# SSD decay exponents and skip term as TensorE products, and four steps stored or moved anew, in a one-core hybrid streaming step

## The chip, the cores and the metric

One core of one Trainium2 chip runs the whole program. The metric is the device time of one execution in microseconds. The kernel before took 1944.94 us (the median of three runs, from 1942.18 to 1947.05).

## The reference, cut to what matters

One layer for 1024 prompt rows and 8 streams of 16 new rows each (nine blocks of 128 rows). Three token mixers read the same projection `u @ w_in`: stick-breaking attention ("sb", 4 heads), forgetting attention ("fox", 4 heads) and a state-space mixer (SSD, 8 heads in 2 groups). Their outputs are put side by side and go through `w_out`; a cross-attention and a SwiGLU FFN follow. The change touches the SSD, the forget-gate sums of the sample rows, and the seam between mixers and `w_out`:

```python
seg = a_cum[:, :, :, None, :] - a_cum[:, :, None, :, :]
decay = jnp.exp(jnp.where(causal[None, None, :, :, None], seg, -jnp.inf))
scores = jnp.einsum('bcthn,bcshn->bctsh', C, B) * decay
y_diag = jnp.einsum('bctsh,bcshp->bcthp', scores, x)
...
y = (y + p['d_skip'].astype(jnp.float32)[:, None] * xs).reshape(b, n, SSD_INNER).astype(u.dtype)
...
fcum = jnp.cumsum(jnp.concatenate([past['fox_logf'].astype(jnp.float32), logf], axis=1), axis=1)
s = s + (jnp.transpose(fq, (0, 2, 1))[..., :, None] - jnp.transpose(fk, (0, 2, 1))[..., None, :])
...
out = jnp.einsum('bne,ed->bnd', mix, p['w_out'])
```

## The kernel before, in words

All is fp32. A large product runs as three TensorE products on a high and a low part of each operand (`mm3`, lines L314, L315, L316); TensorE transposes by a product with the identity. Each engine (PE, DVE, ACT, POOL) works its instructions strictly in the order in which a scheduler put them before the run, from the order and priorities of the code; SP issues every DMA, in one order too, and an issue that waits holds up those behind it. On-chip tiles come from pools with few slots: `ring` has three slots each for tags `wh` and `wl` (two for `wr`), `psd`, `pss`, `pst` are PSUM banks (2, 2, 3), `sgp` has four slots, `actp` six large ones. A tile whose pool is full waits until the last reader of the slot's former owner is done.

The stages in order: memory projection, norm and first projections (to about 120 us of the profile); the attention pipeline, in which the units of the sb heads and then the fox heads run, each pair of streams of the sample rows as one decode unit between them; beside the pipeline, step by step at a set rate, the generator `fill` gives PE other work: first the remaining projections (`fill_s`), and from about 545 us on the SSD (`ssd_gen`). `heads_out` starts with `w_out` beside the last steps, `finish_rows` adds the SSD's part, and cross-attention and FFN follow from 880 us to the end.

The places that the change touches:

- **Sample gate sums**, `fox_sums` in `fill_s`. Running sums of 32 rows (stream, head) over 1024 past and 16 new places are made by scans on DVE (L687), written to DRAM as `fs_sc` with 16 copies of each row (`fssc<-xc`), and read back by each fox decode unit as a bias. A last small product with `hsel` (L696) needs a DVE result (`so`, L692). Then `z_proj` and others follow (L314 to L316 with 264 columns).
- **SSD chunk.** Nine chunks, the sample chunk 8 first, then 0 to 7, each in four parts. `load(i)`: x, B, C of the chunk from `xbc_sc` (L998), the running sums of the gate, 8 heads of 128 values, broadcast to 128 partitions from `ac_sc` (L1000, `act<-acsc`, 512 KB written), and z (L1002). `prepare`: transposes (L1015, L1019), then products with per-head columns on POOL (`heads_tt`, L991), the skip term `xD` with `hb` among them. `weights`: B·C per group on PE (L1030), times the causal mask on DVE (L1032); the difference of running sums, clamped at zero, per head on ACT (L1038, 3 heads) or DVE (L1040, 5 heads); the exponential on ACT (L1043); times the masked B·C on DVE (L1046). `states`: the state's part of y and the new state (L1055, L1061; in chunk 8 per stream, L1092 to L1108, from two loads `act<-state_ssm` of 1024 KB that are issued there). Its last line adds xD on POOL. `outputs`: the products with x (L1118), the sum (L1120), times z on POOL, the norm (L1125). `write`, one chunk late: four transposes (L1130) and two stores to `mix_sc` (L1134).
- **Fox decode.** K of two streams comes in halves through `wr`, is transposed (L856) and copied by ACT (L857) into `kf`, tags `wh` and `wl` of the ring; V comes in halves as `vr` straight into the same two tags (L905), read by 64 small products (L896: 32 for each unit, beside 4 with the new rows).
- **The seam.** `load_rows` brings the heads' rows from `mix_sc` (L1311) when the last of them are stored (L596 stores one head's part); `add_rows` walks the nine blocks with four k each, `act<-mixsc` (L1320) brings the SSD's part.

Of the kernel before, what the change touches and what calls it, by code (L numbers as in the profile page):

```python
# [8 lines left out]
F32 = mybir.dt.float32  # L9
# [8 lines left out]
P = 128  # L18
# [22 lines left out]
NACT = 3  # L41
FSC, CBE = "D", "DD"
# [20 lines left out]
def tile_hybrid_step(ctx: ExitStack, tc: tile.TileContext, a: dict):  # L63
# [177 lines left out]
    fs_sc = dram([32, DEC_S, PAST + DEC_S], F32, "fssc")  # L241
    ac_sc = dram([72, P], F32, "acsc")
# [403 lines left out]
    def fox_sums():  # L646
# [164 lines left out]
    def decode_units(m):  # L811
# [15 lines left out]
        def rows(p):  # L827
# [47 lines left out]
            SP.dma_start(out=fkb[:, :PAST], in_=fs_sc[8 * p:8 * p + 8, :, :PAST].rearrange("i t k -> (i t) k"))  # L875
# [51 lines left out]

    def ssd_gen():
# [8 lines left out]
        avx = sc[:, 1944:2456]  # L937
        ndsk = hb[:, 20:28]
# [37 lines left out]
        at = sg2_t()  # L976
        DVE.tensor_copy(at[:72, :P], ps[:72, :P])
        SP.dma_start(out=ac_sc, in_=at[:72, :P])
# [16 lines left out]

        def load(i):
# [3 lines left out]
            SP.dma_start(out=A[:, 1024:2048],  # L1000
                         in_=ac_sc[8 * i:8 * i + 8, :].rearrange("h t -> (h t)").unsqueeze(0).to_broadcast([P, 1024]))
# [8 lines left out]
        def prepare(i, A, B):  # L1010
# [12 lines left out]
            heads_tt(xD, xn, ndsk)  # L1023

        def weights(i, A, B):
            xT, br, zt, Bn, cb, xn, xd, xe, xD = views(A, B)

            ps = pd()
            for g in range(2):
                PE.matmul(ps[:, g * P:(g + 1) * P], xT[:, 4 + g, :], xT[:, 6 + g, :], start=True, stop=True)  # L1030
            msk = triu if i < 8 else btri
            DVE.tensor_tensor(out=cb.rearrange("p (g t) -> p g t", g=2), in0=ps[:, :256].rearrange("p (g t) -> p g t", g=2),  # L1032
                              in1=msk.unsqueeze(1).to_broadcast([P, 2, P]), op=ALU.mult)

            for h in range(8):
                e, a_s = br[:, h * P:(h + 1) * P], acum[:, 8 * i + h:8 * i + h + 1]
                if h < NACT:
                    ACT.activation(e, e, AF.Relu, bias=a_s, scale=-1.0)  # L1038
                else:
                    DVE.tensor_scalar(e, e, a_s, 0.0, ALU.subtract, ALU.min)  # L1040
            for h0, h1, sgn in ((0, NACT, -1.0), (NACT, 8, 1.0)):
                if h1 > h0:
                    ACT.activation(br[:, h0 * P:h1 * P], br[:, h0 * P:h1 * P], AF.Exp, scale=sgn)  # L1043
            for g in range(2):
                b3 = br[:, g * 512:(g + 1) * 512].rearrange("p (h t) -> p h t", h=4)
                (DVE if CBE[g] == "D" else POOL).tensor_tensor(out=b3, in0=b3, in1=cb[:, g * P:(g + 1) * P].unsqueeze(1).to_broadcast([P, 4, P]),  # L1046
                                  op=ALU.mult)

        def states(i, A, B, t1):
# [14 lines left out]
            else:  # L1064
                hs_, cps = [], []
                for g in range(2):
                    t = act_t(F32)
                    hst = t[:, :2048].rearrange("p (u n) -> p u n", n=P)
                    SP.dma_start(out=hst, in_=a["state_ssm"][0, 4 * g:4 * g + 4].rearrange("b h p n -> (b h p) n")
                                 .rearrange("(u p) n -> p u n", p=P))  # L1070
# [41 lines left out]
            pool_tt(t1, t1, xD, ALU.add)  # L1112

        def outputs(i, A, B, t1):
            xT, br, zt, Bn, cb, xn, xd, xe, xD = views(A, B)
            ps = pd()
            for h in range(8):
                PE.matmul(ps[:, h * 64:(h + 1) * 64], br[:, h * P:(h + 1) * P], xd[:, h * 64:(h + 1) * 64],  # L1118
                          start=True, stop=True)
# [19 lines left out]
        B = act_t(F32)  # L1139
        prepare(order[0], A, B)  # L1140
# [3 lines left out]
        for n, i in enumerate(order):  # L1144
# [20 lines left out]
            last = (i, t1)  # L1165
            if n < 8:
# [4 lines left out]
        write(*last)  # L1171
# [750 lines left out]
```

## Time and profile before

| quantity | value |
|---|---|
| three runs | 1942.18, 1944.94, 1947.05 us |
| the profiled execution, its own time | 1950.47 us |
| its span in the profile | 1948.8 us |
| its mean granted TensorE clock | 0.979 |
| DMA moved in 560 to 760 us | 51.94 MB |
| DMA `act<-acsc` | 9 of 512 KB each |
| DMA `fssc<-xc` | 1 of 2080 KB |

The profile's page gives busy time by engine and, in 40 slices, how busy each is and which TensorE clock was granted. The table of windows does the same for any stretch of time. The waits of PE name, for each line, what ended the idle time ahead of it. The groups by line and form give count, busy time and mean of one, and the idle time before them by what ended it. The chain that ended last follows the run back from its end; a piece of it is the time in which nothing else could have been late. PE overlaps neighbouring instructions, so what a product costs is the distance between the starts of two, not its duration; an fp32 product that isn't one of the three rounded parts leaves two records.

### The profile page before, as it was taken

The numbers are of one execution on the slowest core, as the hardware profiler recorded it, in microseconds if no ns is written. First come the engines' busy times: TensorE is split into PE (matmuls) and PEld (weight loads), VectorE is DVE, ScalarE is ACT, GpSimd is POOL, SyncE is SP. The second block draws the span as 40 slices with busy tenths as digits, with TensorE's granted clock in tenths as the row PEclk, the third lists the DMA queues.
The fourth block names the chain that finished last, engine by engine and source line by source line (L and its number), as shares of the span: only waits on it lengthen the run. The fifth ranks groups of instructions, "written<-read, shape, count | busy, mean of one in ns | idle before, by whom it ended". The sixth has DMA issues, their size and how long they took to land.

```text
span 1948.8 us, 32126 instructions
## 1 busy us (share of the span) xinstructions
PE 1848.2 (95%) x12128; PEld 1647.8 (85%) x12128; DVE 898.4 (46%) x1802; ACT 818.2 (42%) x1702; POOL 629.8 (32%) x918
## 2 busy tenths in 40 slices
PE   7989997999888888999999999999999999999997
PEld 5889776898876665889998888999999999888886
DVE  3421324466645883254444377433333333445554
ACT  6431543445656772143333165333332333344443
POOL 6632405263424552321101212644444443000000
PEclk9999997999999898999999999999999999999999
DMA  9355756445487789234559123332223323556572
GB/s 340 130 168 153 218 122 155 132 137 166 137 241 239 240 273 331 87 115 141 166 165 367 64 96 99 98 74 68 69 68 95 75 68 87 193 189 232 180 243 88
DMA packets 325754, 307.52 MB, mean 158 GB/s; under 512 B 88540, under 2 KB 288324, under 8 KB 325600
## 3 DMA queue, kind: packets, MB, share of 16 engines
q1 hardware_dynamic: 325600, 305.48, 51.2%
q8 instruction: 95, 1.56, 0.3%
q14 instruction: 59, 0.48, 0.1%
HBM read 229.31 MB, written 76.11 MB: 157 GB/s over the span
## 4 chain that ended last, share of the span: by engine, by line
PE 78%; DMA 6%; DVE 4%; POOL 2%; ACT 2%; issue 1%; SPq 0%; DVEq 0%; POOLq 0%; ACTq 0%
PE psd L1789 11%; PE psd L314 10%; PE psd L315 10%; PE psd L316 10%; PE pst L1789 8%; PE pss L1789 4%; PE pss L314 2%; PE pss L315 2%; PE pss L316 2%; PE pso L1789 2%; PE pst L314 2%; PE pst L315 2%; PE pst L316 2%; PE pso L580 1%; PE pst L856 1%
## 5 line engine op out<-in xcount | busy, mean ns | idle before, releaser
L132 POOL TENSOR_TENSOR wl<-wr,wh 128x256 fp32r<-128x256 f32 (+1 forms) x180 | 139.4, 808 | 241.1 <-ACT wh L289 185.0
L314 PE MATMUL psd<-act,wh 128*128 128x384 f32 x576 | 197.7, 344 | 5.3 <-DVE sg L441 2.6
L315 PE MATMUL psd<-act,wh 128*128 128x384 f32 x576 | 196.7, 341 | 0.0
L316 PE MATMUL psd<-act,wl 128*128 128x384 f32 x576 | 196.4, 341 | 0.1
L1789 PE MATMUL pst<-bT,tr 128*128 128x256 f32 (+1 forms) x1068 | 155.0, 293 | 0.0
L316 PE MATMUL psd<-wh,act 128*128 128x512 f32 (+3 forms) x464 | 152.5, 330 | 0.0
L314 PE MATMUL psd<-wh,act 128*128 128x512 f32 (+3 forms) x446 | 146.8, 333 | 4.3 <-ACT wh L289 1.9
L315 PE MATMUL psd<-wl,act 128*128 128x512 f32 (+3 forms) x446 | 146.6, 329 | 0.0
L1789 PEld LDWEIGHTS pst<-bT,tr 128*128 128x128 f32 x1068 | 144.9, 188 | 0.1
L1789 PE MATMUL psd<-bT,tr 128*128 128x320 f32 (+1 forms) x912 | 133.2, 295 | 0.8 <-DVE tr L1636 0.5
L251 POOL TENSOR_SCALAR sm<-sm 128x1 f32<-128x1 f32 (+2 forms) x30 | 11.0, 368 | 378.3 <-ACT y L1884 291.5
L1789 PEld LDWEIGHTS psd<-bT,tr 128*128 128x128 f32 x912 | 124.7, 188 | 1.8 <-DVE tr L1636 0.7
L314 PEld LDWEIGHTS psd<-act,wh 128*128 128x128 f32 x576 | 108.7, 189 | 9.4 <-DVE sg L441 3.0
L132 POOL TENSOR_TENSOR tr<-u,tr 128x256 fp32r<-128x256 f32 x110 | 82.6, 780 | 101.1 <-ACT tr L1632 83.3
L132 POOL TENSOR_TENSOR ws<-ws 128x256 f32<-128x256 f32 (+2 forms) x100 | 73.0, 759 | 116.3 <-DVE ws L507 86.6
L316 PEld LDWEIGHTS psd<-act,wl 128*128 128x128 f32 x576 | 108.5, 188 | 2.0 <-issue 1.3
L315 PEld LDWEIGHTS psd<-act,wh 128*128 128x128 f32 x576 | 108.8, 189 | 0.9 <-issue 0.6
L1764 DVE TENSOR_TENSOR tr<-tr,pst 128x256 f32<-128x256 f32 (+1 forms) x86 | 38.6, 449 | 139.4 <-ACT tr L1761 106.1
L314 PEld LDWEIGHTS psd<-wh,act 128*128 128x128 f32 x446 | 85.6, 192 | 14.2 <-ACT wh L289 2.1
L132 POOL TENSOR_TENSOR tr<-raw,tr 128x256 fp32r<-128x256 f32 x94 | 69.4, 768 | 84.6 <-ACT tr L1632 76.4
L316 PEld LDWEIGHTS psd<-wh,act 128*128 128x128 f32 x464 | 89.0, 192 | 8.7 <-issue 1.3
L289 ACT CAST wh<-wr 128x1024 fp32r<-128x1024 f32 (+2 forms) x45 | 47.1, 1051 | 111.3 <-PE psd L316 48.1
(590 smaller groups left out, 4617.4 us busy)
## 6 DMA issues: line engine op xcount, KB each, us to landing
u<-w_down SPq DMA_DIRECT2D x40, 512.0 KB
raw<-w_down SPq DMA_DIRECT2D x26, 512.0 KB
st<-qksc SPq DMA_DIRECT2D x48, 256.0 KB
wr<-w_in SPq DMA_DIRECT2D x22, 512.0 KB
tr<-hidsc SPq DMA_DIRECT2D x57, 192.0 KB
hidsc<-tr SPq DMA_DIRECT2D x34, 288.0 KB
qksc<-sg SPq DMA_DIRECT2D x48, 192.0 KB
wr<-cache_sb_k SPq DMA_DIRECT2D x16, 512.0 KB
```

The source lines that it names most:

```text
L132: POOL.tensor_tensor(out=out[:, a0:a1], in0=in0[:, a0:a1], in1=in1[:, a0:a1], op=op)
L251: POOL.tensor_scalar(v, ss, inv, EPS, ALU.mult, ALU.add)
L289: ACT.copy(hi[:, :n], raw[:, :n])
L314: PE.matmul(out, ah, bh, start=start, stop=False)
L315: PE.matmul(out, ah, bl, start=False, stop=False)
L316: PE.matmul(out, al, bh, start=False, stop=stop)
L580: return PE.matmul(po[r:r + 64, q_], vt[:, 2 * (k0 + i) + j, :], pfs[i][:, sl], start=start and k0 == 0 and (j == 0 or qp > 0), stop=k0 + ...
L856: PE.transpose(tp[:, k * P:(k + 1) * P], rv[:, k, nb * P:(nb + 1) * P], ident)
L1764: DVE.tensor_tensor(out=at(out, g), in0=at(x, g), in1=ps[g][:, :GW[g]], op=op)
L1789: PE.matmul(dst[g][:, :GW[g]], x[:, ka], y[:, k, :], start=start and k == 0 and m == 0, stop=stop and k == 3 and m == 2, skip_group_check= ...
```

## The change

- `fox_sums` writes two copies of each row instead of 16 (260 KB for 2080 KB) and the decode units read them with a broadcast; after the scan and the stores it hands PE four steps of `z_proj(0)` before its last product.
- SSD decay. The negated running sums are split in a high and a low part and stored to `ac_sc`. Per chunk three small loads bring them to `mv` (10 rows of 1024) and `kv` (10 rows of 256), beside rows of ones and indicators loaded once from the new `ind_sc`. Per group of four heads PE makes the exponent in a `pst` bank: one product puts the mask there (512 columns), one of depth 10 adds the differences (512 columns). ACT takes the exponential straight from PSUM, DVE multiplies with B·C, which stays in its `psd` bank (`cp`). L1032, L1038, L1040 and the broadcast load go. `mv` takes two of the three `wh` slots of the ring for the length of the SSD, `kv` and the sample mask one of the three `wl` slots.
- Skip term. POOL builds diag(d_skip) once (4 operations); per chunk four fp32 products of 128 x 128 put the skip term into the bank of y, and the eight products with x add to it. 18 operations of L991 and 18 additions on POOL go.
- The states of the 8 streams come in eight loads of 256 KB right behind the loads of the first chunk instead of two of 1024 KB in `states`.
- The last chunk's `write` is put off until 12 more steps of `heads_out` have been given out; `add_rows` runs the first two k of a block three blocks ahead of its last two, in banks of `psd` and `pss` in turn.

```diff
-        SP.dma_start(out=fs_sc, in_=sr.unsqueeze(1).to_broadcast([32, DEC_S, PAST + DEC_S]))
+        SP.dma_start(out=fs_sc, in_=sr.unsqueeze(1).to_broadcast([32, 2, PAST + DEC_S]))
         for p in range(4):
             SP.dma_start(out=fqs[:, p:p + 1], in_=fs_sc[8 * p:8 * p + 8, 0, PAST:PAST + DEC_S])
+        yield
+        for _ in range(NZ):
+            yield next(z)
...
+        mv = [ring.tile([P, 1056], F32R, tag="wh", name="wh")[0:10, :1024] for _ in range(2)]
+        cr = ring.tile([P, 1056], F32R, tag="wl", name="wl")
+        kv = [cr[0:10, 256 * x:256 * x + 256] for x in range(2)]
+        mask8 = cr[:, 512:640]
...
-            SP.dma_start(out=A[:, 1024:2048],
-                         in_=ac_sc[8 * i:8 * i + 8, :].rearrange("h t -> (h t)").unsqueeze(0).to_broadcast([P, 1024]))
+            SP.dma_start(out=f32(mv_[0:2]), in_=f32(ac_sc[:, 8 * i:8 * i + 8, :].rearrange("x h t -> x (h t)")))
+            for x in range(2):
+                SP.dma_start(out=f32(kv_[2 + 4 * x:6 + 4 * x]).rearrange("h (g t) -> h g t", g=2),
+                             in_=f32(ac_sc[x, 8 * i:8 * i + 8, :]).rearrange("(g h) t -> h g t", h=4))
...
-            heads_tt(xD, xn, ndsk)
...
-                if h < NACT:
-                    ACT.activation(e, e, AF.Relu, bias=a_s, scale=-1.0)
+                if i < 8:
+                    PE.matmul(p3, mask_fx, identr.unsqueeze(1).to_broadcast([P, 4, P]), start=True, stop=False)
                 else:
-                    DVE.tensor_scalar(e, e, a_s, 0.0, ALU.subtract, ALU.min)
...
+                PE.matmul(ps, sums[i][1][:, g * P:(g + 1) * P], sums[i][0][:, sl], start=False, stop=True)
...
+                ACT.activation(br[:, sl], pss_[g], AF.Exp)
...
-            pool_tt(t1, t1, xD, ALU.add)
...
+            for j in range(4):
+                PE.matmul(ps[:, j * P:(j + 1) * P], xT[:, j, :], skip[:, j * P:(j + 1) * P], start=j == 0, stop=False,
+                          skip_group_check=True)
...
+        st8 = [act_t(F32) for _ in range(2)]
+        for b in range(8):
+            SP.dma_start(out=st8[b // 4][:, 512 * (b % 4):512 * (b % 4 + 1)].rearrange("p (u n) -> p u n", n=P),
+                         in_=a["state_ssm"][0, b].rearrange("h p n -> (h p) n").rearrange("(u p) n -> p u n", p=P))
...
+            if n == 8:
+                final.append(lambda: write(i, t1))
...
-        write(*last)
-        yield
...
+        zs = [z_proj(i) for i in range(2)]
+        yield from fox_sums(zs[0])
...
+            for blk in range(NBLK + ahead):
+                if blk < NBLK:
+                    half(blk, 0)
+                    yield
+                if blk >= ahead:
+                    half(blk - ahead, 2)
+                    yield
...
+    for _ in range(12):
+        next(ho, None)
+    final[0]()
```

The order of instructions on PE behind the small product of `fox_sums` (L685 before), in the kernel before. L547, L548 and L550 are scores of an sb head; L696 is the last small product, L756 belongs to the padding that follows:

```order
L685 MATMUL psd<-fold,so 32x16
L547 MATMUL pss<-st 128x128
L548 MATMUL pss<-st 128x128
L550 MATMUL pss<-mask_sb,identr 128x128
L547 MATMUL pss<-st 128x256
L548 MATMUL pss<-st 128x256
L550 MATMUL pss<-mask_sb,identr 128x128
L547 MATMUL pss<-st 128x384
L548 MATMUL pss<-st 128x384
L550 MATMUL pss<-mask_sb,identr 128x128
L696 MATMUL psd<-so,hsel 128x128
```

The same place on PE in the changed kernel, tiles numbered; `wh_3090` and `wl_3091` are the first weight unit of `z_proj(0)`, `wh_3101` and `wl_3102` the second:

```order
L314 MATMUL psd_3109<-wh_3090,act_350 128x264
L547 MATMUL pss_3351<-st_3141,st_3140 128x128
L548 MATMUL pss_3351<-st_3142,st_3140 128x128
L550 MATMUL pss_3351<-mask_sb_123,identr_119 128x128
L315 MATMUL psd_3109<-wl_3091,act_350 128x264
L316 MATMUL psd_3109<-wh_3090,act_351 128x264
L314 MATMUL psd_3109<-wh_3101,act_350 128x264
L547 MATMUL pss_3366<-st_3141,st_3140 128x256
L548 MATMUL pss_3366<-st_3142,st_3140 128x256
L550 MATMUL pss_3366<-mask_sb_123,identr_119 128x128
L314 MATMUL psd_3169<-wh_3090,act_350 128x264
```

Between the 32 x 16 product and the first that reads `wl_3102`, 26 products of `z_proj` now stand among the head's scores; before, all of them stood behind L696.

The second fox decode unit of those that run beside the SSD, on PE in the kernel before (L896 reads the V halves, L1030, L1055, L1061 are the SSD's):

```order
L1030 MATMUL psd<-act 128x128 x2
L1055 MATMUL psd<-act 128x256 x2
L896 MATMUL pso<-pt,act 32x128 x4
L896 MATMUL pso<-vr,act 32x128 x32
L1061 MATMUL psd<-act 128x256 x2
```

The same unit on PE in the changed kernel (L902 is the line that was L896; L1154 are the skip products, L1157 those with x, L1169 the transposes of `write`, L1071 the B·C products):

```order
L902 MATMUL pso<-pt,act 32x128 x4
L902 MATMUL pso<-vr,act 32x128 x17
L1154 MATMUL psd<-act 128x128 x4
L1157 MATMUL psd<-act 128x64 x8
L1169 MATMUL psd<-ident,sg 128x128 x4
L902 MATMUL pso<-vr,act 32x128 x15
L1071 MATMUL psd<-act 128x128 x2
```

The 32 products of one piece have become 17 and 15 with work of the SSD between them; three of the four fox decode units are split so.

More of the change, by code (lines that the diff above doesn't have):

```diff
@@ L975, in ssd_gen @@
         PE.transpose(ps[:72, :P], acum, ident)
-        at = sg2_t()
-        DVE.tensor_copy(at[:72, :P], ps[:72, :P])
-        SP.dma_start(out=ac_sc, in_=at[:72, :P])
+        t = sg2_t(F32R)
+        an = [t[0:72, P * x:P * x + P] for x in range(2)]
+        ACT.activation(an[0], ps[:72, :P], AF.Copy, scale=-1.0)
+        DVE.scalar_tensor_tensor(an[1], ps[:72, :P], -1.0, f32(an[0]), ALU.mult, ALU.subtract)
+        for x in range(2):
+            SP.dma_start(out=f32(ac_sc[x]), in_=f32(an[x]))
+        DVE.tensor_scalar(mask8, btri, -1.0, -NEG, ALU.add, ALU.mult)
+        for j in range(4):
+            POOL.tensor_tensor(out=skip[:, j * P:(j + 1) * P].rearrange("p (h d) -> p h d", d=64),
+                               in0=ident.rearrange("p (h d) -> p h d", d=64),
+                               in1=ndsk[:, 2 * j:2 * j + 2].unsqueeze(2).to_broadcast([P, 2, 64]), op=ALU.mult)
         POOL.memset(hT, 0.0)
@@ L994, in heads_tt @@
                                    op=ALU.mult)
+        sums, loads = {}, [0]
         def load(i):
@@ L1035, in weights @@
-            for h in range(8):
-                e, a_s = br[:, h * P:(h + 1) * P], acum[:, 8 * i + h:8 * i + h + 1]
-                if h < NACT:
-                    ACT.activation(e, e, AF.Relu, bias=a_s, scale=-1.0)
-                else:
[L1040 to L1043, printed above, removed]
+                PE.matmul(cp[:, g * P:(g + 1) * P], xT[:, 4 + g, :], xT[:, 6 + g, :], start=True, stop=True)
@@ L1065, in states @@
                 hs_, cps = [], []
-                for g in range(2):
-                    t = act_t(F32)
+                for g, t in enumerate(st8):
                     hst = t[:, :2048].rearrange("p (u n) -> p u n", n=P)
-                    SP.dma_start(out=hst, in_=a["state_ssm"][0, 4 * g:4 * g + 4].rearrange("b h p n -> (b h p) n")
-                                 .rearrange("(u p) n -> p u n", p=P))
                     cp = t[:, 2048:3072]
@@ L1252, in tile_hybrid_step, with add_rows @@
             acc -= 1.0
-    def add_rows(w, k0, rows, h):
+    def add_rows(w, k0, rows, h, ahead=0):
         for j in range(2):
@@ L1328, in heads_out @@
         more_h(NBLK)
-        yield from add_rows(a["w_out"][0], 0, lambda k, b: [t[:, b * P:(b + 1) * P] for t in rows[k]], h)
+        yield from add_rows(a["w_out"][0], 0, lambda k, b: [t[:, b * P:(b + 1) * P] for t in rows[k]], h, 3)
     ho = heads_out()
     weave(fill, ho, WV, "ho")
+    for _ in range(12):
+        next(ho, None)
+    final[0]()
     ch = [chunk_t() for _ in range(NCH)]
```

67 lines of the change are left out of this document (43 added, 24 removed).

## The prediction

> **What bounds the kernel now.** I read the page first: who is busy, and what the chain that ended last is made of.
>
> ```profile
> span 1948.8 us, 32126 instructions
> PE 1848.2 (95%) x12128; PEld 1647.8 (85%) x12128; DVE 898.4 (46%) x1802; ACT 818.2 (42%) x1702; POOL 629.8 (32%) x918
> PE 78%; DMA 6%; DVE 4%; POOL 2%; ACT 2%; issue 1%; SPq 0%; DVEq 0%; POOLq 0%; ACTq 0%
> ```
>
> TensorE is busy 95% of the span and holds 78% of the chain; no other engine comes near it. So work that is added to PE costs its full price except where PE stands still or is slowed, and work that is taken from DVE, ACT, POOL or DMA gains only where PE waits for it. Hence the windows next: where does PE stand still?
>
> ```profile
> core 0: us, PE busy (x) PEld busy (x) DVE busy (x) ACT busy (x) POOL busy (x), PEclk, DMA share, GB/s
> 312.00:320.00 8.00, 7.87 (x44) 7.75 (x43) 2.68 (x6) 1.76 (x5) 5.78 (x12) 0.57 0.98 199
> 566.00:576.00 10.00, 4.90 (x25) 4.60 (x25) 3.77 (x12) 4.12 (x10) 4.31 (x6) 0.66 0.95 281
> 616.00:618.00 2.00, 2.00 (x11) 2.00 (x11) 1.08 (x6) 0.61 (x2) 1.68 (x7) 0.50 1.10 303
> 580.00:747.00 167.00, 147.73 (x1200) 111.36 (x1198) 120.47 (x338) 116.12 (x255) 87.16 (x138) 0.95 0.82 257
> 747.00:764.00 17.00, 9.38 (x30) 6.76 (x30) 3.89 (x10) 2.33 (x6) 5.76 (x10) 0.70 0.99 323
> 1180.00:1949.00 769.00, 755.52 (x4797) 704.31 (x4796) 340.01 (x585) 282.61 (x556) 228.71 (x312) 0.99 0.41 121
> ```
>
> The long last stage (FFN) has PE busy throughout at full clock, and the change leaves it alone. The chunks of the SSD, 580 to 747 us, are different: PE is busy 147.73 of 167 us, so 19.3 us idle, and at a granted clock of 0.95, which is another 7.4 us (5% of 147.73) lost to a slow clock. These 26.7 us are all that this stretch can give. Around it lie three short holes (from 304, at 566, at 747 us), each followed by a stretch at a low clock. Whom PE waits for there, the waits say:
>
> ```profile
> PE psd L696 <- DVE so L692: 6.4, 1, 6.4
> PE pst L1092 <- DMA act<-state_ssm: 4.8, 1, 4.8
> PE psd L1130 <- DVE sg L1125: 4.2, 1, 4.2
> PE pst L856 <- DMA wr<-cache_fox_k: 3.8, 2, 2.8
> PE pso L896 <- DMA vr<-cache_sb_v: 3.6, 2, 1.9
> PE psd L1015 <- DMA act<-xbcsc: 3.0, 3, 1.7
> PE psd L1055 <- DVE act L1032: 2.9, 3, 1.7
> PE psd L314 <- DMA ws<-mixsc: 2.7, 1, 2.7
> PE pss L547 <- ACT xc L686: 1.3, 1, 1.3
> ```
>
> Each of the four moves aims at one of these rows: the sums at L696, the states at L1092, the last write at L1130 and `ws`; the SSD's new exponent does away with L1032.
>
> **The gate sums.** PE stood 6.4 us before L696 and 1.3 us before L547. What follows it ran on a half clock:
>
> ```profile
> 313.49 0.42 PE L315 MATMUL psd<-wl,act 128*128 128x264 f32 x1
> 313.71 0.42 PE L316 MATMUL psd<-wh,act 128*128 128x264 f32 x1
> ```
>
> One 264-column product then starts each 0.22 us. The order puts 26 of them ahead of the second weight unit's low part, 26 x 0.22 = 5.7 us of work out of the slow stretch into the hole. They cannot close it: the second unit's low half is made on POOL behind operations that wait for the same DVE scans, so PE stands still again until about where it did. From nothing (the products find no operands in time) to all of hole and slow clock (6.4 + 1.3 + 7.87 x 0.43 = 11.1), I take 5, somewhat less than the 5.7. The smaller store, 260 KB for 2080 KB, shortens a DMA that no row here waits for: nothing; the cover is the time until the first fox decode unit, and if that were gone it could gain, not lose.
>
> **The states.** Hole 4.8 us, slow clock after it 4.90 x 0.34 = 1.7: 6.5 at most. The wait goes, but what is late next stands in the same queue:
>
> ```profile
> 561.79 9.88 DMA act<-state_ssm
> 219.10 7.97 DMA vr<-cache_sb_v
> 743.13 7.95 DMA mixsc<-sg
> 751.13 7.09 DMA ws<-mixsc
> ```
>
> A load takes 7 to 10 us when the engines are full (DMA share 0.95 in the window of 566). The 2 MB now go ahead on SP of the indicator store, its four loads, the store of the split sums and the small loads, and the first exponent product waits for that whole chain. I take a gain of 1, between a loss of 2 and 6.5.
>
> **The seam.** The last head's store and its load back take 7.95 + 7.09 = 15 us in the chain, whatever PE does. In that time the changed order has 15 products of `w_out` before the first that reads that head, where 9 stood, and the four skip products of the last chunk: 6 x 0.23 + 4 x 0.23 (both prices below) = 2.3 us of cover gained; the bounds are nothing and the whole hole with its clock (4.2 + 2.7 + 9.38 x 0.30 = 9.7). The deferred write is hidden behind some hundred products of `w_out`.
>
> **The SSD on PE.** Per chunk two mask and two exponent products of 512 columns, and four fp32 products of 128 x 128. Prices, from neighbours of the same shape:
>
> ```profile
> 748.02 0.39 PE L315 MATMUL psd<-wl,ws 128*128 128x512 f32 x1
> 748.25 0.39 PE L316 MATMUL psd<-wh,ws 128*128 128x512 f32 x1
> 663.77 0.46 PE psd L1030 x4
> ```
>
> One starts 0.23 us after the other; and four records of L1030, which are two products, hold the chain for 0.46, so 0.23 each. 36 x 0.23 + 36 x 0.23 = 16.6 us added to PE. What lies beside idle time: PE's pieces in the chain between 580 and 747 us come to about 67 of 167 us, 40% (my sum over its pieces; five of them are quoted in this part and the ring's). By that share 6.6 us land on the path and 10 are hidden; the bounds are nothing and 16.6.
>
> **What the SSD's other engines lose.**
>
> ```profile
> L1040 DVE TENSOR_SCALAR act<-act 128x128 f32<-128x128 f32 x45 | 15.0, 394 | 5.0 <-DMA act<-acsc 5.0
> L1038 ACT ACTIVATE act<-act 128x128 f32<-128x128 f32 x27 | 9.2, 394 | 8.6 <-DMA act<-acsc 8.5
> L1032 DVE TENSOR_TENSOR act<-psd,act 128x256 f32<-128x256 f32 x9 | 3.7, 414 | 2.6 <-PE psd L1030 2.6
> L991 POOL TENSOR_TENSOR act<-act,hb 128x256 f32<-128x256 f32 x18 | 10.9, 628 | 0.0
> L132 POOL TENSOR_TENSOR sg<-sg,act 128x256 f32<-128x256 f32 x36 | 27.8, 794 | 40.9 <-ACT ws L517 12.7 <-DVE sg L1057 12.1 <-DVE sm L525 5.4
> act<-acsc SPq DMA_DIRECT2D x9, 512.0 KB
> 696.30 1.43 POOL sg L132 x2
> ```
>
> DVE is rid of 15.0 + 3.7 us, ACT of 9.2, POOL of 10.9 and half of 27.8, DMA of 9 x 0.5 = 4.6 MB, a ninth of what the stretch moves (257 GB/s x 167 us = 43 MB). What of this reaches PE: the 2.9 us at L1055 for L1032; half of the waits for `cache_fox_k` and `xbcsc` (3.8 + 3.0), 3.4; with fewer holes half of the slow clock, 3.7; and some of the pairs of L132 that stand in the chain at 1.43 us, of which the removed ones are half of the 18, 2. Together 12; the bounds are the 2.9 alone and the 26.7 of the stretch less the 10 above, 16.7. The exponential's input from PSUM, not SBUF, has no row here; the sizes stay near each other and I put it at nothing, with ACT's 9.2 us as cover.
>
> **The ring.** This speaks against the change. With two of three `wh` slots held, a fox decode unit has one: its second V half can be loaded only when the first has been read. The order shows it, 17 products, other work, 15. Before, no fox V wait shows among PE's waits; the nearest row is that of the sb units, 3.6 in two, the longest 1.9. Three units at 1.9 make 5.7, my value. The upper bound: a load of 7.97 us as in the chain above, less the work that the order has put between, priced by
>
> ```profile
> 607.96 1.93 PE psd L1118 x16
> 662.95 0.82 PE psd L1130 x4
> 593.24 0.86 PE psd L1103 x2
> 730.23 0.87 PE psd L1055 x4
> ```
>
> The first unit has 4 x 0.23 of scores and 0.86; the second 4 x 0.23, 1.93 and 0.82; the third 0.82, 2 x 0.23 and 0.87: in all 7.6 us, so 3 x 7.97 - 7.6 = 16.3, and with a slow clock after each (1.7 as after the states) 21.4. The lower bound is the sb units' 3.6. Last, a `psd` bank held through the exponentials and two `pst` banks shared with the transposes of K: 1, between nothing and the 2.9 that the bank cost at L1055.
>
> One rule belongs here. PE stood 2.83 us before this row, and the window of 616 shows 0.50 behind it:
>
> ```profile
> 615.77 1.32 PE L856 MATMUL pst<-ident,wr 128*128 128x128 f32 x5 [2.83 <-DMA wr<-cache_fox_k]
> ```
>
> The Trainium skill, TensorE: Matmul & The Clock Gate, Part 1: The HAM clock gate, has the clock fall to half after an idle window of about 3.4 us and rise after as long a busy one. By that rule waits of 1.9 us cost no clock and the ring's term is 5.7; by the row, where 2.83 us sufficed, each might cost 1.7 more, the term would be 10.8, and the time below 1943. I keep 5.7, since 1.9 is under both.
>
> **The sum**, against the profiled execution's own 1950.47 us: -5 - 1 - 2.3 + 16.6 - 10 - 12 + 5.7 + 1 = -7.0, so 1943.5. That execution is 5.5 us above the median of the three runs (1944.94); at the median's level 1938.0. A measurement of this kernel can tell about 0.3% from no change, 5.8 us: faster is under 1939.1, slower over 1950.8.
>
> **The rivals.**
>
> A larger gain, 0.20. PE's new products all fall into idle time and the ring's waits are covered: 6.6 + 5.7 less, -19.3, 1926; if both holes close as well (6.1 and 7.4 more), 1912. For it: every engine but PE is under 75% in the stretch. Against: it needs more than the 26.7 us of slack that the stretch has.
>
> No change, 0.14. All of PE's 16.6 us lie on the path, 10 more than taken: +3.0, 1948. For it: PE has 88% of the stretch. Against: the removed waits let the chains run ahead.
>
> Slower, 0.18: the ring. Three V halves wait 7.97 us, each less its work, and PE restarts cold: 21.4 in place of 5.7, +8.7, 1954. The point: the sum passes +5.8 when the ring costs 18.5, that is at a load of 7.0 us with the slow clock (3t - 7.6 + 5.1), or 8.7 without. For it: DMA share 0.82, loads of 7 to 10 us in the chain. Against: the DMA queue loses 4.6 MB, and while PE stands the chains catch up.
>
> That the change does not do what it says can be true of the sums: the products in the hole may wait for the same POOL; that is the lower end of that term, 1943.
>
> **How the numbers follow.** My forecast, 0.48, is 1938, its own range 1930 to 1946 (half of the distance to the ends of the terms, partly cancelling); 0.30 of it lies under 1939.1, 0.18 above. With the larger gain's 0.20: faster 0.50. Same: 0.18 and 0.10 of the no-change case, 0.28. Slower: the ring's 0.18 and 0.04 of that case, 0.22. The range reaches from near the larger gain's far end, 1914, to just beyond the ring's case, 1957.
>
> **What the profile would show.** Right: L696's wait small and 26 products ahead of it; no wait for `state_ssm`; waits for `vr<-cache_fox_v` of about 2 us, three times; PE's busy time up by some 16 us (less where the clock was slow before) and the stretch 580 to 747 about as long as it was; the hole at 747 two us shorter. Wrong: V waits of 4 us and more with a low clock behind them; the first exponent product late by more than the states were; PE's idle time in the chunks not lower, which would put all of its new work on the path; or the stretch shorter by 10 us, which would mean that the chains and not PE set it.

## The result, and the profile after

The changed kernel takes 1954.15 us (median of 6 runs, 1950.3 to 1955.13), the kernel before 1945.84 (6 runs): a ratio of 1.004, 95% interval 1.0022 to 1.0058. It is slower by 8.3 us. I had forecast 1938 and faster; the slow case had 0.22.

Single executions of either kernel scatter by several microseconds, and the two profiled ones lie on opposite sides of their medians: before's 4.6 us above (1950.47), after's 2.8 below (1951.36). So the traces tell where time went, and the timed runs, each beside runs of the kernel before on the same chip, tell how much. The page of the kernel after:

```profile
span 1949.6 us, 32288 instructions
PE 1867.5 (96%) x12236; PEld 1657.8 (85%) x12236; DVE 881.3 (45%) x1752; ACT 811.4 (42%) x1676; POOL 603.6 (31%) x886
PE 77%; DMA 4%; DVE 4%; ACT 1%; POOL 1%; issue 1%; SPq 0%; ACTq 0%; DVEq 0%; POOLq 0%
```

DVE, ACT and POOL did less, as foreseen, by 17.1, 6.8 and 26.2 us. PE is busy 19.3 us longer, at a better clock. The same windows as of before:

```profile
312.00:320.00 8.00, 7.15 (x59) 6.96 (x58) 3.62 (x8) 3.30 (x8) 6.21 (x12) 1.00 0.39 115
566.00:576.00 10.00, 6.39 (x42) 4.42 (x43) 4.90 (x19) 6.86 (x17) 4.62 (x6) 0.94 0.65 204
580.00:747.00 167.00, 156.53 (x1186) 114.39 (x1186) 96.31 (x280) 103.58 (x216) 51.37 (x96) 1.00 0.73 221
747.00:764.00 17.00, 15.62 (x154) 12.68 (x152) 4.51 (x9) 5.80 (x12) 10.93 (x17) 1.00 0.86 290
1180.00:1949.00 769.00, 754.88 (x4789) 703.35 (x4788) 336.53 (x579) 281.93 (x555) 228.90 (x312) 0.99 0.41 121
```

All holes at the places I had named shrank, and among the chunks (580 to 747) the granted clock is 1.00 and PE's idle time 10.5 us, not 19.3: 16 of the 26.7 us of slack were won. The window is one of fixed times, though, and the same work ends later: the last attention product at 750.6 us, before at 740.5. With less waiting, PE must have more to do than my sum gave it. Behind the first hole, moreover, the clock became worse. The stretch from 325 to 480 us, first before, then after:

```profile
325.00:480.00 155.00, 148.75 (x1089) 132.90 (x1088) 79.93 (x135) 69.31 (x155) 54.43 (x79) 0.99 0.47 139
```

```profile
325.00:480.00 155.00, 146.90 (x999) 128.56 (x999) 78.51 (x126) 67.37 (x146) 59.02 (x77) 0.94 0.44 127
```

At 0.94 PE loses 8.8 us there (146.90 x 0.06), at 0.99 it lost 1.5: these 7 us are more than the wait of 6.4 us that went at L696. Some of the waits of PE in the kernel after:

```profile
PE pso L902 <- DMA vr<-cache_sb_v: 6.2, 2, 4.4
PE pst L860 <- DMA wr<-cache_fox_k: 4.5, 5, 1.3
PE pst L1080 <- DMA wl<-acsc: 2.9, 1, 2.9
PE psd L315 <- POOL wl L131: 2.3, 1, 2.3
PE psd L314 <- DVE so L737: 2.1, 1, 2.1
PE psd L314 <- ACT xc L724: 1.8, 1, 1.8
PE psd L314 <- DMA ws<-mixsc: 1.4, 1, 1.4
PE pso L902 <- DMA vr<-cache_fox_v: 1.3, 1, 1.3
```

Three things stand here. The wait at the gate sums' last product is gone, but the next sb unit's V now waits 4.4 us (longest before: 1.9), and three waits of about 2 us are new; one of them, for `wl` from POOL, I had foreseen. The states' wait of 4.8 has become 2.9 us at the first exponent product (L1080). And the rival of the ring did not come: `cache_fox_v` shows once, 1.3 us.

What PE does more of is seen in its timeline, start first, in a chunk of the kernel after:

```profile
654.60 0.48 PE L1077 MATMUL pst<-identr,mask_fx 128*128 128x512 f32 x1
655.00 0.50 PE L1080 MATMUL pst<-wh,wl 10*128 10x512 f32 x1
655.43 0.50 PE L1077 MATMUL pst<-identr,mask_fx 128*128 128x512 f32 x1
655.86 0.50 PE L1080 MATMUL pst<-wh,wl 10*128 10x512 f32 x1
656.29 0.48 PE L1101 MATMUL psd<-act 128*128 128x256 f32 x1
```

Four products hold PE for 1.69 us, 0.42 each; I had taken 0.23. Summed from start to start over the trace, at full clock, the 16 prompt masks cost 6.9, the two sample masks 0.5, the 18 exponents 7.4 and the 36 skip products 8.4: 23.2 us for my 16.6. The skip products cost what I had taken, 0.23 each (8.4 / 36); the whole error lies in the masks and exponents, 14.8 us for my 8.3. The K products of the sample units (L848) cost 3.9 more than before: in two of the fox pieces the four parts of a product, whose starts are 7 ns apart elsewhere, no longer stand together in the order. No run shows what split them.

### The profile page after: what moved, and what is told of

Its sections match the earlier page's. It is cut to its first block, busy times and chain, and to the rows that moved or that the text cites. A ratio compares the mean times of both kernels' runs of the same rounds, so it can differ in the third digit from the quotient of the medians.

```text
span 1949.6 us, 32288 instructions
## 1 busy us (share of the span) xinstructions
PE 1867.5 (96%) x12236; PEld 1657.8 (85%) x12236; DVE 881.3 (45%) x1752; ACT 811.4 (42%) x1676; POOL 603.6 (31%) x886
## 4 chain that ended last, share of the span: by engine, by line
PE 77%; DMA 4%; DVE 4%; ACT 1%; POOL 1%; issue 1%; SPq 0%; ACTq 0%; DVEq 0%; POOLq 0%
PE psd L1845 11%; PE pst L1845 8%; PE psd L314 8%; PE psd L315 8%; PE psd L316 8%; PE pss L1845 4%; PE pss L314 3%; PE pss L315 3%; PE pss L316 3%; PE pso L1845 2%; PE pso L580 2%; PE pst L314 1%; PE pst L315 1%; PE pst L316 1%; PE pst L565 1%; PE pst L860 1%
## 5 line engine op out<-in xcount | busy, mean ns | idle before, releaser
L315 PE MATMUL psd<-act,wh 128*128 128x384 f32 x576 | 197.7, 343 | 0.0
L316 PE MATMUL psd<-act,wl 128*128 128x384 f32 x576 | 197.3, 343 | 0.2 <-POOL wl L131 0.2
L314 PE MATMUL psd<-wh,act 128*128 128x256 f32 (+3 forms) x414 | 133.4, 325 | 4.6 <-ACT wh L289 1.8
L316 PE MATMUL psd<-wh,act 128*128 128x512 f32 (+3 forms) x424 | 136.5, 323 | 0.0
L315 PE MATMUL psd<-wl,act 128*128 128x256 f32 (+3 forms) x414 | 133.6, 323 | 2.4 <-POOL wl L131 2.3
L315 PEld LDWEIGHTS psd<-act,wh 128*128 128x128 f32 x576 | 109.3, 190 | 1.2 <-issue 1.0
L316 PEld LDWEIGHTS psd<-act,wl 128*128 128x128 f32 x576 | 109.2, 190 | 1.2 <-POOL wl L131 0.7
L314 PEld LDWEIGHTS psd<-wh,act 128*128 128x128 f32 x414 | 78.8, 191 | 13.2 <-issue 2.4
L1688 ACT CAST tr<-tr 128x384 fp32r<-128x384 f32 (+1 forms) x70 | 37.7, 538 | 125.0 <-DMA tr<-hidsc 120.4
```

Source lines behind the costliest of these rows:

```text
L314: PE.matmul(out, ah, bh, start=start, stop=False)
L315: PE.matmul(out, ah, bl, start=False, stop=False)
L316: PE.matmul(out, al, bh, start=False, stop=stop)
L1688: ACT.copy(hi, src)
```

## The experiments

Times are medians. Each ratio is to runs of the kernel before that were timed beside it; their medians were 1945.9 to 1947.4 us, and 1943.5 beside seam_copies and seam_dec.

**The price of the exponent (rows128).** The operands are filled up to 128 rows with zeros.

```diff
-        mv = [ring.tile([P, 1056], F32R, tag="wh", name="wh")[0:10, :1024] for _ in range(2)]
+        mv = [ring.tile([P, 1056], F32R, tag="wh", name="wh")[:, :1024] for _ in range(2)]
...
-        kv = [cr[0:10, 256 * x:256 * x + 256] for x in range(2)]
+        kv = [cr[:, 256 * x:256 * x + 256] for x in range(2)]
+        for t in (mv[0], mv[1], cr[:, :512]):
+            POOL.memset(f32(t), 0.0)
```

> The changed kernel, with the operands of the exponent product filled up with zero rows to the full 128 partitions; the result is the same. In the changed kernel's trace the mask product and the exponent product, which stand in turn, start 0.42 us apart, not 0.23 as I had taken from the products of 512 columns in the seam. Price theory: the product of 10 rows and the one of 128 rows do not overlap, each change of shape costs about 0.19 us; with one shape the 34 products cost 0.23 each and the kernel comes out 5 to 7 us under the changed one (about 1947 to 1949). Pattern theory: it is the repeated operand (the identity read four times over), so the pitch stays at 0.42 and the time at 1954. Ring theory: PE's price is not what made it slower, the time stays within 2 us of the changed kernel, whatever the pitch.

1944.63 us, ratio to before 0.9991 (0.9975 to 1.0007): 9.5 us under the changed kernel. Its timeline in the same chunk:

```profile
649.31 0.48 PE L1079 MATMUL pst<-identr,mask_fx 128*128 128x512 f32 x1
649.63 0.39 PE L1082 MATMUL pst<-wh,wl 128*128 128x512 f32 x1
649.86 0.39 PE L1079 MATMUL pst<-identr,mask_fx 128*128 128x512 f32 x1
650.09 0.39 PE L1082 MATMUL pst<-wh,wl 128*128 128x512 f32 x1
650.32 0.38 PE L1103 MATMUL psd<-act 128*128 128x256 f32 x1
```

Zeros on 118 more rows make the same four products 1.01 us, not 1.69: 0.23 between equals, 0.32 for the first, which follows a product of another form. The repeated operand is the same, so the pattern theory falls. Over the trace, masks and exponents cost 10.4 us, not 14.8: a saving of 4.4, less than the 9.5 of the runs. The mean granted clock of the runs is 0.9874 against 0.9860, worth some 2.7 us more (0.0014 x 1950); the rest is within the two intervals and not accounted for.

**The order of the four (order).**

```diff
-                PE.matmul(ps, sums[i][1][:, g * P:(g + 1) * P], sums[i][0][:, sl], start=False, stop=True)
                 pss_.append(ps)
+            for g in range(2):
+                sl = slice(g * 512, (g + 1) * 512)
+                PE.matmul(pss_[g], sums[i][1][:, g * P:(g + 1) * P], sums[i][0][:, sl], start=False, stop=True)
```

> The changed kernel with each chunk's products in the order mask, mask, exponent, exponent, all 10-row operands kept. Price theory (a change between a product of 128 rows and one of 10 rows costs some 0.19 us): half of the changes inside a chunk go, the second mask and the second exponent product start 0.23 us after the first, PE saves about 3.4 us and the time is 1949 to 1952. If a 10-row product is slow by itself, only the mask products get cheaper. If the price does not matter, 1954.

1948.53 us, ratio 1.0011 (1.0 to 1.0022). The scheduler put mask, mask, exponent, exponent in two chunks of eight only. There:

```profile
650.94 0.71 PE L1077 MATMUL pst<-identr,mask_fx 128*128 128x512 f32 x2
651.58 0.73 PE L1083 MATMUL pst<-wh,wl 10*128 10x512 f32 x2
652.24 0.48 PE L1103 MATMUL psd<-act 128*128 128x256 f32 x1
```

1.30 us for the four: a pair of equal 10-row products takes 0.66, not 0.46 and not 0.84. So a change between 128 and 10 rows costs about 0.1 us on each side of it. A 10-row product with equal neighbours on both sides does not occur, so whether it would reach 0.23 is not shown. Over the trace the new order saves 0.7 us, which does not explain the 5.6 us that the runs are below the changed kernel; the two intervals just touch (at 1.0022), and I leave that open.

**The skip term (skip_pool).**

```diff
+            heads_tt(xD, xn, ndsk)
...
+            pool_tt(t1, t1, xD, ALU.add)
...
-            for j in range(4):
-                PE.matmul(ps[:, j * P:(j + 1) * P], xT[:, j, :], skip[:, j * P:(j + 1) * P], start=j == 0, stop=False,
-                          skip_group_check=True)
```

> The changed kernel with the skip term back on POOL (18 products with the column, 18 additions) and without its 36 TensorE products, which cost 8.4 us of PE in the trace of after. If PE's work lies on the path at full price, it comes out 8 us under the changed kernel, 1946; if POOL's work was what the chunks waited for, it comes out no faster than the changed kernel, 1954 or above; 40 percent on the path, as I predicted, less 2 us for POOL's pairs in the chain: 1 to 3 us faster, 1951 to 1953.

1947.8 us, ratio 1.0011 (0.9997 to 1.0024): 6.4 us under the changed kernel. By the medians 8.4 us of PE were on the path at three quarters of their price, and POOL's 36 operations come back for little. The interval and that of the changed kernel (1.0022 to 1.0058) overlap slightly, so the share is rough.

**Both (both)**: the two edits above together, rows128 and skip_pool.

```diff
+        for t in (mv[0], mv[1], cr[:, :512]):
+            POOL.memset(f32(t), 0.0)
...
+            heads_tt(xD, xn, ndsk)
```

> The changed kernel with the exponent's operands filled to 128 rows and the skip term back on POOL. If the price of PE's work is what the change paid with, the two gains add (9.5 and 6.4 us in the runs so far): about 1938, faster than the kernel before by 0.3 to 0.5 percent. If the two take the same slack, or POOL's work then sets the chunks, it is no better than the better of the two: 1944 or above.

1942.91 us, ratio 0.9985 (0.9972 to 0.9998). 11.2 us under the changed kernel, not 16: the two take partly the same slack. It just beats the kernel before.

**The ring (hold).** In the kernel before:

```diff
+        held = [ring.tile([P, 1056], F32, tag=x, name="held") for x in ("wh", "wh", "wl")]
+        for t in held:
+            POOL.memset(t[0:10, 0:8], 0.0)
...
+                if n == 7:
+                    for t in held:
+                        POOL.tensor_copy(sc[0:10, 2456:2464], t[0:10, 0:8])
```

> The kernel before, with two of the three wh slots and one of the three wl slots of the ring held from the start of the SSD to its last chunk by tiles that nobody needs (three small memsets and three small copies added). Ring theory: fox K and V wait for the one slot left, their groups of four products are split, and the time rises by 6 us or more, to 1952 or above. Price theory: the ring costs little because other work fills the waits, under 3 us, 1946 to 1949.

1946.8 us, ratio 0.9997 (0.9983 to 1.0011). But the run does not test the ring. POOL's part of its trace shows the copies that were to keep the slots until the last chunk, each right behind its memset:

```profile
553.46 0.10 POOL L941 MEMSET held<- 10x8 f32 x1 [8.03 <-PE psd L316]
553.62 0.18 POOL L1174 COPY act<-held 10x8 f32<-10x8 f32 x1
553.86 0.10 POOL L941 MEMSET held<- 10x8 f32 x1
554.02 0.18 POOL L1174 COPY act<-held 10x8 f32<-10x8 f32 x1
```

The last of the three copies runs at 554.30 us, before the first chunk, so the slots were not held, and the V products of each fox unit stand in one piece as before. Neither theory can be told from this run. What is known of the ring comes from the trace of the changed kernel, where the slots are held: one V wait of 1.3 us, and waits for `cache_fox_k` of 4.5 us in all against 3.8.

**The three moves (moves).** The kernel before with the change's edits to gate sums, states and seam; the SSD as before.

```diff
+        for _ in range(NZ):
+            yield next(z)
...
+        st8 = [act_t(F32) for _ in range(2)]
...
+                final.append(lambda: write(i, t1))
```

> The kernel before with the three moves alone: gate sums stored in two copies with four steps of z_proj ahead of the last product, states loaded early, last SSD write put off with the first two k of w_out three blocks ahead. Decay exponents and skip term stay as before. If the moves gain what the profile of after shows in idle time and clock at their three places (7 to 15 us), it comes out at 1931 to 1939, and the SSD part of the change costs what is between that and 1954. If the holes only moved, it stays at 1946. My prediction's own terms give 8.3 us, 1937.5.

1945.47 us, ratio 0.9994 (0.9983 to 1.0005): together they gain nothing. So each went alone.

**The seam (seam).**

```diff
+            if n == 8:
+                final.append(lambda: write(i, t1))
...
+            for blk in range(NBLK + ahead):
...
+    for _ in range(12):
+        next(ho, None)
+    final[0]()
```

> The kernel before with the late write of the last chunk and the w_out products three blocks ahead, nothing else. My prediction gave 2.3 us of gain. The stretch from the last attention product to the start of cross-attention is 9 to 12 us shorter in every trace that has this move, so if that is its own doing: 8 us or more, 1938 or below. If that stretch only got shorter because other work had been pushed ahead of it: no gain, 1944 to 1947.

1935.98 us, ratio 0.9945 (0.9927 to 0.9964): 9.9 us faster alone. From the last attention product to one of the transposes that make the FFN's operands (the 57th of 72, the same in all three), in the kernel before (chain, timeline), after, and in this one:

```profile
739.47 1.08 PE pso L580 x7
```

```profile
1172.88 0.33 PE L1685 MATMUL pst<-ident,st 128*128 128x128 f32 x1 [0.49 <-ACT u L1676]
```

```profile
749.48 1.08 PE L580 MATMUL pso<-pt,st 128*64 128x256 f32 x8
...
1169.95 0.33 PE L1741 MATMUL pst<-ident,st 128*128 128x128 f32 x1 [0.50 <-ACT u L1732]
```

```profile
736.66 1.08 PE L580 MATMUL pso<-pt,st 128*64 128x256 f32 x8
...
1160.15 0.66 PE L1699 MATMUL pst<-ident,st 128*128 128x128 f32 x4 [0.49 <-ACT u L1690]
```

1172.88 - 740.55 = 432.3 us before, 419.4 after, 422.4 here, 9.9 less than before. I took 2.3, and the upper bound was the whole hole with its slow clock, 9.7. The gain has that size, but the hole did not close. The wait at the last chunk's transposes (L1130 before, 4.2 us) is gone, the one for the last head is not:

```profile
PE psd L314 <- DMA ws<-mixsc: 3.4, 1, 3.4
```

Between the two marks PE's idle time is 4.5 us against 11.2, and the half clock lasts 6.8 us against 10.2, which is worth 1.7. Six products of `w_out` now stand ahead of the last attention product, at 0.23 another 1.4. Together that is 9.8 of the 9.9. In all 36 products of `w_out` stand ahead of the one that waits for the last head, before it was 9.

**The gate sums (sums, late, sums_ny, copies, zonly).** The whole move in the kernel before:

```diff
-        SP.dma_start(out=fs_sc, in_=sr.unsqueeze(1).to_broadcast([32, DEC_S, PAST + DEC_S]))
+        SP.dma_start(out=fs_sc, in_=sr.unsqueeze(1).to_broadcast([32, 2, PAST + DEC_S]))
...
+        yield
+        for _ in range(NZ):
+            yield next(z)
```

> The kernel before with the gate sums' move alone (two copies stored, four steps of z_proj ahead of the last small product). My prediction gave this a gain of 5. Moved-hole theory: the hole of 6.4 us before the last product closes, but the traces with this move have new waits in its place (4.4 us for the V of the next sb decode unit, and 1.8 and 2.1 us at the padding of the convolution, each with 3.5 us or more of half clock), so it gains nothing: within 3 us of the kernel before, 1943 to 1949. Gain theory: 1939 to 1942.

1955.4 us, ratio 1.0049 (1.003 to 1.0068): 9.5 us slower, where I had a gain of 5. The bare `yield` alone:

```diff
+        yield
```

> The kernel before with one bare step more in the gate sums and nothing else: the step does no work, but the generator that feeds PE beside the attention pipeline is one step behind from there on, so the SSD begins one pipeline step later (its first transposes stand at row 2607 of PE's order, not 2577) and more of it is left when the attention ends. Step theory: this alone makes the 9.5 us by which the gate sums' move was slower: 1952 or above. Wait theory: the loss comes from the new waits (V of the second sb unit, padding) behind the moved products; the bare step costs under 3 us, 1949 or below.

1950.28 us, ratio 1.0015 (0.9997 to 1.0033): between the two cases, and by its interval not to be told from the kernel before. The move without it:

```diff
+        for _ in range(NZ):
+            yield next(z)
```

> The gate sums' move without the bare step: two copies stored, four steps of z_proj ahead of the last product; the SSD begins at row 2574 of PE's order, as before. Step theory: the loss of 9.5 us is gone and what the closed hole is worth shows, 1940 to 1947. Wait theory: it stays at 1952 or above.

1954.93 us, ratio 1.0047 (1.003 to 1.0064). So the step theory falls: the loss stays without the step. The copies alone:

```diff
-    fs_sc = dram([32, DEC_S, PAST + DEC_S], F32, "fssc")
+    fs_sc = dram([32, 2, PAST + DEC_S], F32, "fssc")
```

> The kernel before with the running sums stored in two copies, not 16, and read with a broadcast; nothing moved. My prediction put this at nothing, since no row waited for the store: 1943 to 1949. If the 2 MB store delayed the V loads behind it, it gains 2 us or more; if the broadcast read of few rows is slower and the sample units wait for it, it loses 3 us or more, and then it is part of the 9.5.

1944.85 us, ratio 0.9985 (0.9968 to 1.0003), no harm. And the moved steps alone, 16 copies, no bare step:

```diff
+        for _ in range(NZ):
+            yield next(z)
```

> The kernel before with four steps of z_proj ahead of the last product of the gate sums, 16 copies and no bare step. If the moved products are what costs (the wait passes to the V of the second sb unit, whose loads stand behind z's stores in SP's queue, and the rest of the order shifts): 1952 to 1957, as the whole move. If it is the two copies together with the steps: 1949 or below.

1956.76 us, ratio 1.0051 (1.0039 to 1.0063): these four steps are the loss. The kernel before reads the V of the next sb unit in two parts with 24 products of z between them, and the loads of the second part are issued when the first has been read (PE, then SP's queue):

```profile
329.11 1.06 PE L896 MATMUL pso<-vr,st 128*32 128x128 f32 x32
335.21 1.31 PE L896 MATMUL pso<-vr,st 128*32 128x128 f32 x32 [1.93 <-DMA vr<-cache_sb_v]
```

```profile
330.21 0.94 SPq L905 DMA_DIRECT2D vr<-cache_sb_v  x2
```

SP's queue and PE's timeline in zonly:

```profile
323.58 2.05 SPq L772 DMA_DIRECT2D zsc<-sg  x2
325.72 1.01 SPq L908 DMA_DIRECT2D vr<-cache_sb_v  x2
```

```profile
322.47 1.06 PE L899 MATMUL pso<-vr,st 128*32 128x128 f32 x32
331.22 1.08 PE L899 MATMUL pso<-vr,st 128*32 128x128 f32 x16 [7.69 <-DMA vr<-cache_sb_v]
```

PE reaches the V products earlier and stands 7.7 us between the two parts, with a half clock behind, where it stood 6.4 us before L696. Two things lengthen the wait from 1.9 us. The 24 products of z that had covered the load, 3.2 us, are now ahead of it; and the loads come 2.2 us after the first part has been read, behind z's stores, where they came at once. That is shown; that it is all of the 9 us is not: the rest of the order shifts with it, and single traces do not resolve the remainder.

**The gate sums in the changed kernel (after_nosums).**

```diff
-        yield
-        for _ in range(NZ):
-            yield next(z)
...
-        yield from fox_sums(zs[0])
+        yield from fox_sums()
```

> The changed kernel with the gate sums as before (16 copies, no z steps ahead, no bare step), all else changed. If the move's price is its own wherever it stands: 9 us under the changed kernel, 1945. If it costs only where the SSD of the kernel before follows, whose leftover after the attention is slow: 0 to 4 us, 1950 to 1954.

1953.8 us, ratio 1.0039 (1.0024 to 1.0055): no difference from the changed kernel. The prices do not add: the move costs 9.5 beside the old SSD and nothing that can be measured beside the new one. Why is not shown.

**The seam in the changed kernel (after_noseam).**

```diff
-                final.append(lambda: write(i, t1))
...
+        write(*last)
+        yield
...
-    for _ in range(12):
-        next(ho, None)
-    final[0]()
```

> The changed kernel with the last write and the order of w_out as before. The seam gained 9.9 in the kernel before; if it is worth the same here, the time rises to 1962 to 1966, and without the seam the change would have cost 18 us. If the SSD's new products take the place that the seam frees, it rises by less than 5 us.

1964.66 us, ratio 1.0082 (1.0066 to 1.0097). The seam is worth 10.5 us here too, and without it the change would have cost 17 (1947.4 beside it).

**The states (states).**

```diff
+        st8 = [act_t(F32) for _ in range(2)]
+        for b in range(8):
+            SP.dma_start(out=st8[b // 4][:, 512 * (b % 4):512 * (b % 4 + 1)].rearrange("p (u n) -> p u n", n=P),
+                         in_=a["state_ssm"][0, b].rearrange("h p n -> (h p) n").rearrange("(u p) n -> p u n", p=P))
```

> The kernel before with the eight early loads of the states alone. My prediction gave a gain of 1 between a loss of 2 and 6.5; as the remainder of the three moves it came to about 0. If the wait of 4.8 us and its slow clock go: 1940 to 1943. If the 2 MB ahead of the chunk's other loads only hand the wait on: 1944 to 1948.

1949.69 us, ratio 1.0009 (0.9996 to 1.0022): no gain. The wait for the states is gone from its trace, and between 540 and 600 us, where the kernel before waits for no K, stands another:

```profile
PE pst L856 <- DMA wr<-cache_fox_k: 4.0, 1, 4.0
```

**What to keep (best, seam_copies, seam_dec).** The changed kernel with 128 rows, skip on POOL and gate sums as before:

```diff
+            heads_tt(xD, xn, ndsk)
...
-        yield from fox_sums(zs[0])
+        yield from fox_sums()
```

> The changed kernel with the exponent's operands in 128 rows, the skip term on POOL and the gate sums as before; states loaded early, last write and w_out as changed. The runs so far: the seam alone is 9.9 us faster than before, decay on PE in 128 rows with skip on POOL is 2.6 us faster than the moves alone, the gate sums' move costs 9.5. If these add: about 1933, faster than both kernels and than the seam alone (1936). If the SSD's PE work eats what the seam frees, 1936 to 1942.

1940.97 us, ratio 0.997 (0.9955 to 0.9985): the second case. The seam and the two copies in the kernel before:

```diff
+    fs_sc = dram([32, 2, PAST + DEC_S], F32, "fssc")
...
+    final[0]()
```

> The kernel before with the seam's part and the two copies of the gate sums, nothing else. If the two gains add (9.9 and 2.1): 1934 to 1935, about 0.6 percent faster than the kernel before. If the copies' 2.1 us was within the error: 1936.

1935.83 us, ratio 0.996 (0.9946 to 0.9973). And best without the early states:

```diff
-                for g, t in enumerate(st8):
+                for g in range(2):
+                    t = act_t(F32)
```

> The seam's part and the decay exponent on PE with 128-row operands; skip term on POOL, gate sums and states as in the kernel before. If the early states were what cost 5 us: 1936 or below. If the decay on PE costs: 1940 to 1943, and even at the lower price the products are not worth the work they take from DVE, ACT and DMA.

1935.74 us, ratio 0.9964 (0.9952 to 0.9977). The intervals of the three and of the seam alone overlap: the decay on PE, even in 128 rows, adds nothing to the seam that can be told apart, and neither do the copies. The price of the early states is not resolved either (best against seam_dec, 0.997 and 0.9964). The seam alone is the fastest by its ratio, 0.55% under the kernel before, and a few lines.

## Why the prediction was wrong

- **PE's price, the step that failed first.** "36 x 0.23 + 36 x 0.23 = 16.6". The second half of it, the skip products, was right (8.4 us). The first was not: the row L315/L316 was of the right width, but its neighbours are of the same form; mask and exponent stand in turn with 128 and 10 rows and cost 0.42 each, 14.8 us for 8.3. In all 23.2 us, and 3.9 for split K products, a term that the sum did not have. rows128 shows what the shape cost: 4.4 us in the trace, 9.5 in the runs.
- **What is hidden.** I let 10 of 16.6 us fall into idle time and 12 more come from relieved chains, 22 of the 26.7 us of slack. Measured: 16 us of slack gone, against 27 us of added work. skip_pool shows a path share of about three quarters (6.4 of 8.4, a rough figure) where I had 40%. That share was read from the chain of the kernel before, 67 of 167 us between 580 and 747; in the changed kernel PE's pieces come to at least 110 of these 167 us, two thirds. With the waits gone the chain is more PE, so the old share was too small for the new work.
- **Relief of DVE, ACT, POOL.** The mechanism was right: clock 1.00 among the chunks, the wait at L1055 for L1032 gone. But the work given to PE costs more than the relief.
- **Gate sums.** "I take 5" failed. I had priced the hole and its clock, and looked for what PE waits for next only at the second weight unit; the next wait was for the V of the next sb unit, 7.7 us in zonly, 4.4 in the changed kernel. The moved products had covered that load, and their stores stand ahead of it in SP's queue; I had asked neither. In the changed kernel the move gains nothing measurable (after_nosums).
- **States.** A gain of 1 taken; none measured. That the wait passes to what is late next in the same queue held: in states a half of `cache_fox_k` takes 4.0 us, in the changed kernel the exponent's small loads 2.9, for the 4.8 that went.
- **Seam.** The sign was right, the size wrong: 10 us, not 2.3. I counted six more products against a fixed 15 us of store and load, and the changed kernel does have those 15 behind the last store. But 12 more stand ahead of the store, 27 in all; and the wait of 4.2 us for the last write went whole. That the gain equals the upper bound is chance, since the wait for the last head stayed in seam (3.4 us).
- **Ring.** The rival for the slow side had the sign and, by chance, the number (1954), but not the cause: V waits were 1.3 us once, for the 18.5 us that it needed. Held slots alone were not measured, since hold did not hold them. The clock rule of the Trainium skill that I weighed there was not put to the test, as those waits did not come.
- **The sum, redone** in the changed kernel: seam -10.5 (after_noseam), gate sums 0 (after_nosums), states about +2 and within error, so the SSD's part is +17, the remainder of 8.3. My terms for it, 16.6 - 10 - 12 + 5.7 + 1, came to +1.3. Of the 17, 11 are shape and skip (both), and some 6 the rest of the decay on PE and its order, which is the difference and not measured by itself; between seam_dec and seam, where shape and skip are out of it, the intervals overlap. The seam's 8 us more than forecast hid part of this: the sum was off by 15 us, from -7.0 to +8.3, and the SSD's part alone by 16.

## What to carry to other kernels

On a kernel whose TensorE is 95% busy, a product is priced from a neighbour in the same sequence and shape, not only of the same width; here a product of 10 rows and its full neighbours cost nearly double, and padding it with zeros took that away for three memsets. When work is moved into a hole, ask what it had covered where it stood and what its stores now stand ahead of in the DMA queue; here the wait reappeared there. Time each part of a joint change alone: here a gain of 10 us was hidden behind losses that were larger. And look in an experiment's own trace whether it did what it was made for: the slots of hold were free again at once.

## What the runs showed of the hardware that I had not expected

A product of 512 columns and 128 rows takes 0.23 us to the next start among equals, about 0.32 with a change between 128 and 10 rows on one side, and 0.42 with one on both (timelines of rows128, order and after). The first behind products of another form also takes 0.32 (rows128); the last ahead of one, with 128 rows on both sides, 0.23. The same wait can cost very different times in slow clock. The same V products waited nearly alike in two kernels; their row in the timeline, and the window of 10.5 us that begins 3 to 4 us later (its last three columns are clock, DMA share and GB/s), first in the kernel after, then in skip_pool:

```profile
326.74 0.44 PE L902 MATMUL pso<-vr,st 128*32 128x128 f32 x4 [4.38 <-DMA vr<-cache_sb_v]
```

```profile
329.50:340.00 10.50, 10.50 (x52) 8.10 (x52) 1.37 (x5) 3.68 (x9) 4.40 (x7) 0.54 0.48 119
```

```profile
328.79 0.32 PE L902 MATMUL pso<-vr,st 128*32 128x128 f32 x4 [4.36 <-DMA vr<-cache_sb_v]
```

```profile
332.50:343.00 10.50, 10.50 (x86) 8.66 (x85) 2.25 (x8) 4.43 (x10) 3.63 (x6) 1.00 0.52 148
```

The first ran on half a clock for another 10.5 us with PE fully busy, the second at full clock: about 4.8 us of difference (10.5 x 0.46) after the same wait. In the clock records of these traces the stretches of half clock last 3.4, 6.8, 10.2 or 13.7 us, in zonly once 17.1: whole multiples of 3.413. The Trainium skill, TensorE: Matmul & The Clock Gate, Part 1: The HAM clock gate, has a free-running window of about 3.4 us; the step of the lengths agrees with it. The Trainium skill has the clock rise, in the table of the same part, after at least one busy window. In the kernel after, PE, busy by the profile, stayed slow for three. Both kernels start the stretch with the same work, V products, transposes and padding, so the work alone does not decide, and no run here shows what does.
